# Second FFN of a one-layer decoder step: seven products in place of eight for two of three token chunks, parts kept in HBM between an up and a down phase

## Chip, cores and metric

One core of a Trainium2 chip. The metric is the device time of one execution in microseconds; of several executions the median counts.

## What is computed

One inference step of one layer, for a prompt of 1024 tokens and 8 single sample tokens, which share the weights: 1032 token rows of 1024 features.

```python
def swiglu(x, w_gate, w_up, w_down):
    return (jax.nn.silu(x @ w_gate) * (x @ w_up)) @ w_down

x = x + 0.5 * swiglu(rms_norm(x, g_ffn1), w1_gate, w1_up, w1_down)
proj = rms_norm(x, g_mix) @ w_in          # S5 branch, dilated attention, two gates
mixed = gate_ssm * (y_ssm @ w_ssm_proj) + gate_attn * (y_attn @ w_attn_proj)
x = x + mixed @ w_o
x = x + 0.5 * swiglu(rms_norm(x, g_ffn2), w2_gate, w2_up, w2_down)
```

The hidden width of both FFNs is 2816. Besides x the step returns key and value caches and S5 states. The change concerns the last line alone.

## The kernel before

Activations are feature-major: a tile xT holds 128 features on the partitions, 8 such blocks (KT), and 344 tokens (CH) in the columns; three chunks of 344 tokens make 1032. A float32 product is made as three matmuls of rounded parts (float32r): every operand is split into a high part (a cast on ScalarE) and a low part (the rest, a subtraction on VectorE), and high x high, high x low and low x high are added in PSUM (`mm3`, L148). Weights come in blocks of 512 KB through `loadw` (L131): a DMA from SP, the cast (L141), the subtraction (L142).

The step runs in stages: first FFN, mix (SSM, attention, gates, output projection `wo`), second FFN. The order of the instructions on each engine is set by a scheduler within the program's dependencies and the numbers of buffers.

In the mix stage's end `wo` (L1138 and following) adds the projection to chunk c of xT, and `wo_norm` (L1145) norms that chunk for the second FFN: squares on ScalarE, their sum over features by additions and one matmul with ones (`pT<-ss`, L120), a reciprocal root (`rsq`, L92), eight scalings (L127), and the split of each (L128, L129). It is called for chunk c right after `wo` of chunk c, so that it can stand beside the projection of the next chunk, or beside the FFN's first products.

`ffn` (L169) goes over 22 blocks f of 128 hidden features. `gateup(f)` makes gate and up products for three chunks: 2 x 8 x 3 x 3 = 144 matmuls of 128x344; the hidden block is split and stays in SBUF. After each pair of blocks `down` adds the pair before to all of xT: 8 x 3 x 2 x 3 = 144 matmuls per pair. The last `down` takes four blocks and goes chunk by chunk, and `store_x` (L939) turns each finished half of a chunk back to token-major by TensorE transposes (L950), copies (L951) and stores; six xr buffers.

## Time and profile before

| | us |
|---|---|
| median of 3 runs | 2418.6 (2417.37 to 2424.5) |
| profiled execution, its span | 2416.6 |
| TensorE busy | 2357.5 |
| VectorE busy | 1185.9 |
| ScalarE busy | 689.0 |
| GpSimd busy | 265.1 |

Of the profiled execution only the span is given; the median of the runs is 2.0 us above it. The second FFN begins at about 1660 us and ends with the kernel. How to read the views: a group gives one line's instructions of one shape with the mean of one; TensorE's matmuls overlap, so that the distance of their starts, not their mean, is what one takes in a stream. The chain of waits follows back, from the last instruction, what released each step.

### The profile page before, as it was taken

What the parts mean: (1) busy time and instruction counts of PE and PEld (TensorE: products, weight loads), DVE (VectorE), ACT (ScalarE), POOL (GpSimd) and SP (SyncE); (2) the same over time, 40 slices, a digit from 0 to 9 for tenths busy, and PEclk for the clock granted to TensorE, in tenths of its full rate; (3) what the DMA queues carried; (4) which work ended last, traced back from release to release, by engine and by line L of the source; (5) the groups of instructions that cost most, each with busy time, mean ns of one, the idle gap of its engine ahead of it and who ended that gap; (6) DMA issues with size and microseconds to landing.
All of it is one profiled execution on the core that took longest, in us unless ns stands there. A gap on an engine that the chain in (4) does not pass through costs nothing.

```text
span 2416.6 us, 37129 instructions
## 1 busy us (share of the span) xinstructions
PE 2357.5 (98%) x14805; PEld 2265.3 (94%) x14805; DVE 1185.9 (49%) x2690; ACT 689.0 (29%) x1364; POOL 265.1 (11%) x811
## 2 busy tenths in 40 slices
PE   7999999999999899989999999899999999999999
PEld 6999999999999799978887887899999999999999
DVE  7655544355442825555575535786234434433333
ACT  6211111111112433555444422345211111111111
POOL 2056766000001300000000000000000000000000
PEclk8999999999999899999999999999999999999999
DMA  5333434333233377551231246653111111111112
GB/s 140 97 111 104 128 95 130 105 94 113 82 110 102 128 202 232 164 157 45 80 108 46 63 135 199 188 159 92 45 43 53 48 40 53 44 44 53 50 39 71
DMA packets 279044, 241.24 MB, mean 100 GB/s; under 512 B 28958, under 2 KB 261054, under 8 KB 276694
## 3 DMA queue, kind: packets, MB, share of 16 engines
q1 hardware_dynamic: 274518, 190.66, 26.5%
q10 hardware_dynamic: 2816, 44.00, 6.0%
q0 software_dynamic: 1536, 4.21, 0.5%
q8 instruction: 116, 1.90, 0.3%
q14 instruction: 58, 0.48, 0.1%
HBM read 202.32 MB, written 80.49 MB: 117 GB/s over the span
## 4 chain that ended last, share of the span: by engine, by line
PE 90%; DMA 5%; DVE 3%; ACT 1%; issue 1%; SPq 0%; POOL 0%; DVEq 0%; ACTq 0%; POOLq 0%
PE pm L156 82%; PE ps L669 2%; DMA rs<-g_d 1%; PE acc L685 1%; PE pT L678 1%; PE pn L978 1%; DMA y_d<-Y 1%; DVE wl L142 1%; DMA num<-s_d 1%; DVE xn L127 0%; DMA raw<-in_w_in_dram 0%; DMA w<-w_d 0%; DMA xr<-in_x_prompt_dram 0%; PE pT L455 0%; PE pT L808 0%
## 5 line engine op out<-in xcount | busy, mean ns | idle before, releaser
L156 PE MATMUL pm<-al,wh 128*128 128x344 f32 x3280 | 1047.4, 323 | 2.1 <-DVE rs L1132 1.9
L156 PE MATMUL pm<-ah,wh 128*128 128x344 f32 x3152 | 1018.9, 323 | 9.3 <-ACT ah L128 3.8
L156 PE MATMUL pm<-ah,wl 128*128 128x344 f32 x2384 | 769.8, 323 | 2.3 <-DVE wl L142 2.3
L156 PEld LDWEIGHTS pm<-al,wh 128*128 128x128 f32 x3280 | 617.2, 189 | 12.8 <-issue 5.5
L156 PEld LDWEIGHTS pm<-ah,wh 128*128 128x128 f32 x3152 | 595.4, 189 | 19.1 <-issue 4.7
L156 PEld LDWEIGHTS pm<-ah,wl 128*128 128x128 f32 x2384 | 451.4, 189 | 9.7 <-issue 4.8
L141 ACT CAST wh<-raw 128x1024 fp32r<-128x1024 f32 (+1 forms) x220 | 220.4, 1009 | 730.6 <-PE pm L156 690.2
L142 DVE TENSOR_TENSOR wl<-raw,wh 128x1024 fp32r<-128x1024 f32 (+1 forms) x220 | 258.4, 1179 | 223.0 <-ACT wh L141 222.6
L198 DVE SCALAR_TENSOR_TENSOR xT<-pm,xT 128x344 f32<-128x344 f32 x480 | 243.9, 515 | 203.3 <-PE pm L156 203.1
L156 PE MATMUL pm<-hh,wh 128*128 128x344 f32 x1056 | 339.5, 322 | 0.0
L156 PE MATMUL pm<-hl,wh 128*128 128x344 f32 x1056 | 338.2, 320 | 0.0
L156 PE MATMUL pm<-hh,wl 128*128 128x344 f32 x1056 | 337.8, 321 | 0.0
L182 DVE TENSOR_TENSOR h<-h,pm 128x344 f32<-128x344 f32 x132 | 67.5, 512 | 450.6 <-PE pm L156 450.6
L156 PE MATMUL pm<-al,wl 128*128 128x344 f32 x832 | 265.1, 319 | 0.0
L156 PEld LDWEIGHTS pm<-hh,wh 128*128 128x128 f32 x1056 | 198.5, 188 | 0.3
L156 PEld LDWEIGHTS pm<-hl,wh 128*128 128x128 f32 x1056 | 198.4, 188 | 0.2
L156 PEld LDWEIGHTS pm<-hh,wl 128*128 128x128 f32 x1056 | 198.2, 188 | 0.1
L183 ACT CAST hh<-h 128x344 fp32r<-128x344 f32 x132 | 63.1, 478 | 333.4 <-DVE h L182 333.4
L156 PEld LDWEIGHTS pm<-al,wl 128*128 128x128 f32 x832 | 156.1, 188 | 0.1
L181 ACT ACTIVATE h<-pm 128x344 f32<-128x344 f32 x132 | 60.1, 456 | 220.8 <-PE pm L156 220.7
L184 DVE TENSOR_TENSOR hl<-h,hh 128x344 fp32r<-128x344 f32 x132 | 68.6, 520 | 40.0 <-ACT hh L183 39.9
L1133 POOL TENSOR_TENSOR rs<-rs,ah 128x344 f32<-128x344 f32 x3 | 2.8, 928 | 601.3 <-DVE rs L1132 601.3
(339 smaller groups left out, 2032.7 us busy)
## 6 DMA issues: line engine op xcount, KB each, us to landing
out_dram<-in_cache_kv_w_dram ACTq DMA_DIRECT2D x64, 512.0 KB
raw<-in_w_gate_dram SPq DMA_DIRECT2D x44, 512.0 KB
raw<-in_w_up_dram SPq DMA_DIRECT2D x44, 512.0 KB
raw<-in_w_down_dram SPq DMA_DIRECT2D x44, 512.0 KB
raw<-in_w_in_dram SPq DMA_DIRECT2D x38, 512.0 KB
raw<-in_w_o_dram SPq DMA_DIRECT2D x24, 512.0 KB
g_d<-gt SPq DMA_DIRECT2D x48, 172.0 KB
rs<-g_d SPq DMA_DIRECT2D x48, 172.0 KB
```

The source lines that it names most:

```text
L141: nc.scalar.copy(h[:, :k], raw[:, :k])
L142: nc.vector.tensor_sub(l[:, :k], raw[:, :k], h[:, :k])
L156: nc.tensor.matmul(p, w[:, kw], a[:, ka], start=first and i == 0, stop=last and i == n - 1)
L181: nc.scalar.activation(h, pg, AF.Silu)
L182: nc.vector.tensor_mul(h, h, pu)
L183: nc.scalar.copy(hh[:, c], h)
L184: nc.vector.tensor_sub(hl[:, c], h, hh[:, c])
L198: nc.vector.scalar_tensor_tensor(xT[c][:, m], p, 0.5, xT[c][:, m], op0=ALU.mult, op1=ALU.add)
L669: nc.tensor.matmul(p[h][:, :nk], qT[hs, s.block(g, b)], kT[hs, ks], start=True, stop=True)
L678: nc.tensor.transpose(pt[:, h, i], sm[:, h, 128 * i:128 * i + 128], s.ident)
L685: nc.tensor.matmul(acc[hs], vx[:, k, hs], P[:, h, i], start=i == 0, stop=i == nb - 1)
L978: nc.tensor.matmul(p2[:, :CH], s.bones, sq, start=True, stop=True)
```

## The change

The two chunks 0 and 1 are taken as the two column halves of a 2 x 2 block product, with the features (up) or the gate and up weights as the row halves, and the Strassen-Winograd form makes its 8 block products with 7, at the price of sums of operands and results. Chunk 2 is multiplied as before. Up: 7 x 4 x 3 = 84 matmuls for chunks 0 and 1 and 48 for chunk 2, 132 per block f instead of 144. Down: 132 instead of 144 per pair of blocks.

- `wo_norm` is called for all three chunks after `mix`, that is behind `wo` of chunk 2 in the program. It stores x to HBM (x_d), scales xT in place and makes nine split operands of 128x1376 columns (B11, B21, B22, T1 to T4 for chunks 0 and 1; D0, D1 for chunk 2). Three subtractions that GpSimd made are on VectorE.
- `wprep` makes for each f the sums S1 to S4 of the weights and splits them.
- `ffn_up` runs all 22 blocks. `second` makes, per pair of blocks, nine split parts of 128x688 and stores them to a new HBM tensor hs_d, 34.9 MB in all.
- `ffn_down` then runs three groups of 4, 4 and 3 pairs, each in nine runs (P1, P2, lo, hi, P4, P5, P6, P7, P3). A run reads its part back through a ring of four slots (`hload`), and adds into SBUF. In the last group the sums are combined, and `out` loads x again from x_d through one buffer y, adds, transposes and stores through two buffers xr.
- The pool of weight blocks `wp` is opened once for the first FFN and once for mix, instead of once for the kernel.

```diff
@@ run @@
             with ExitStack() as c4:
                 xT, tmp = s.mix(psum, c4)
-                psum(c4, 6, 2)
-                hpc = ExitStack()
-                hp = pool(hpc, "hp2", 4)
-                s.ffn(hp, tmp, i['w2_gate'], i['w2_up'], i['w2_down'], xT, lambda c, m: s.store_x(tmp, xT, c, m))
-                while copies:
-                    shift()
-                hpc.close()
+                s.ep = pool(ctx, "ep", side="right")
+                with ExitStack() as c5:
+                    s.wq = pool(c5, "wq", side="right")
+                    psum(c5, 6, 2)
+                    s.wprep(i['w2_gate'], i['w2_up'])
+                    for c in range(NCH):
+                        s.wo_norm(tmp, xT, c)
+                    c4.close()
+                    with ExitStack() as c6:
+                        s.ffn_up(pool(c6, "up2"))
+            with ExitStack() as c7:
+                psum(c7, 6, 2)
+                s.ffn_down(pool(c7, "wd", side="right"), pool(c7, "yo"), i['w2_down'])
+            while copies:
+                shift()
...
@@ mix @@
                 s.wo(tmp2, xT, 0)
                 s.attn_proj(tmp, oh, ol, 2)
-                s.wo_norm(tmp2, xT, 0)
                 for c in (1, 2):
                     s.wo(tmp2, xT, c)
-                    s.wo_norm(tmp2, xT, c)
         return xT, tmp2
...
+    SLOT = {'B11': 'al1', 'B21': 'ah2', 'B22': 'al2', 'T1': 'ah0', 'T2': 'e0', 'T3': 'e1', 'T4': 'e2', 'D0': 'ah1', 'D1': 'al0'}
+    def slot(s, name, sh, dt):
+        return (s.ep if name[0] == 'e' else s.act).tile(sh, dt, name=name)
+    def parts(s, x, hi, lo):
+        s.nc.scalar.copy(hi, x)
+        s.nc.vector.tensor_sub(lo, x, hi)
     def wo_norm(s, tmp, xT, c):
-        s.ah[c], s.al[c] = (s.act.tile([128, KT, CH], F32R, name=nm) for nm in (("al1", "ah2"), ("al2", "ah0"), ("ah1", "al0"))[c])
-        s.norm(tmp, c, 2, xT, s.ah, s.al)
+        nc = s.nc
+        V = nc.vector
+        nc.sync.dma_start(s.x_d[c], xT[c])
+        ss = tmp.tile([128, CH], F32, name="ss", bufs=1)
+        for k in range(KT):
+            if k == 0:
+                nc.scalar.activation(ss, xT[c][:, k], AF.Square)
+            else:
+                sq = tmp.tile([128, CH], F32, name="sq", bufs=2)
+                nc.scalar.activation(sq, xT[c][:, k], AF.Square)
+                V.tensor_add(ss, ss, sq)
+        p = s.pt.tile([128, 512], F32, name="pT")
+        nc.tensor.matmul(p[:, :CH], s.ones, ss, start=True, stop=True)
+        r = s.rsq(tmp, p[:, :CH], 1.0 / D)
+        for k in range(KT):
+            V.scalar_tensor_tensor(xT[c][:, k], xT[c][:, k], s.gains[:, 2, k:k + 1], r, op0=ALU.mult, op1=ALU.mult)
+        lo, hi = xT[c][:, 0:4], xT[c][:, 4:8]
+        def put(name, x):
+            s.ops[name] = t = s.slot(s.SLOT[name], [128, 2, 4, CH], F32R)
+            s.parts(x, t[:, 0], t[:, 1])
+        if c == 0:
+            s.ops, s.xn0 = {}, (lo, hi)
+            put('B11', lo)
+            put('B21', hi)
+        elif c == 1:
+            b11, b21 = s.xn0
+            V.tensor_sub(b11, lo, b11)
+            V.tensor_sub(lo, hi, lo)
+            put('B22', hi)
+            V.tensor_sub(hi, hi, b11)
+            put('T2', hi)
+            V.tensor_sub(b21, b21, hi)
+            put('T3', lo)
+            put('T1', b11)
+            put('T4', b21)
+        else:
+            put('D0', lo)
+            put('D1', hi)
...
+    def wprep(s, wg, wu):
...
+            put(('A11', 'A12'), g, "wg", 2)
+            V.tensor_add(S[0][:, 0:4], u[:, 0:4], u[:, 4:8])
+            V.tensor_sub(S[0][:, 4:8], S[0][:, 0:4], g[:, 0:4])
+            put(('S1', 'S2'), S[0], "wr", 1)
+            V.tensor_sub(S[1][:, 0:4], g[:, 0:4], u[:, 0:4])
+            V.tensor_sub(S[1][:, 4:8], g[:, 4:8], S[0][:, 4:8])
+            put(('S3', 'S4'), S[1], "wt", 1)
+            put(('A21', 'A22'), u, "wu", 1)
...
+    def ffn_up(s, ap):
...
+        def second(j, h1, h2):
+            def put(i, n, x):
+                t = ap.tile([128, 2, 2, CH], F32R, name="hs", bufs=2)
+                s.parts(x, t[:, :n, 0], t[:, :n, 1])
+                nc.sync.dma_start(s.hs_d[i:i + n, j].rearrange("i p z n -> p i (z n)"),
+                                  t[:, :n].rearrange("p i z n -> p i (z n)").bitcast(F32))
+            put(4, 2, h1[:, 0::2])
+            yield 1
+            T = ap.tile([128, 4, CH], F32, name="hT", bufs=1)
+            V.tensor_sub(T[:, 0], h1[:, 1], h1[:, 0])
+            V.tensor_sub(T[:, 1], h2[:, 1], T[:, 0])
+            yield 1
+            put(0, 2, T[:, 0:2])
+            yield 1
+            V.tensor_sub(T[:, 2], h2[:, 1], h1[:, 1])
+            V.tensor_sub(T[:, 3], h2[:, 0], T[:, 1])
+            yield 1
+            put(2, 2, T[:, 2:4])
+            yield 1
+            put(6, 2, h2[:, 0:2])
+            yield 1
+            put(8, 1, h2[:, 2:3])
...
+            a, b, c, d = bank(), None, None, None
+            s.mmk(a, W['A11'], O['B11'], 4)
+            p1 = u("p1")
+            nc.scalar.copy(p1, a)
+            b = bank()
+            s.mmk(b, W['S2'], O['T2'], 4)
+            U = u("U")
+            V.tensor_add(U, b, p1)
+            d = bank()
+            s.mmk(d, W['S3'], O['T3'], 4)
+            v = u("v")
+            V.tensor_add(v, d, U)
+            c = bank()
+            s.mmk(c, W['S1'], O['T1'], 4)
+            c22 = u("c22")
+            V.tensor_add(c22, c, v)
+            s.mmk(a, W['A12'], O['B21'], 4, False)
+            sl = u("sl", 2)
+            nc.scalar.activation(sl, a, AF.Silu)
+            s.mmk(d, W['A22'], O['T4'], 4, False)
+            c21 = u("cc", 2)
+            V.tensor_add(c21, d, U)
+            V.tensor_mul(h[:, 0], sl, c21)
+            s.mmk(c, W['S4'], O['B22'], 4, False)
+            c12 = u("cc", 2)
+            V.tensor_add(c12, c, U)
+            nc.scalar.activation(c12, c12, AF.Silu)
+            V.tensor_mul(h[:, 1], c12, c22)
...
+            if f % 2:
+                todo.append(second(f // 2, prev, h))
+            prev = h
+        step(20)
...
+    def ffn_down(s, wd, yo, w):
...
+        def hload(name, js):
+            nm = ('al2', 'e0', 'e1', 'e2')[hn[0] % 4]
+            hn[0] += 1
+            t = s.slot(nm, [128, 4, 2, CH], F32R)
+            nc.sync.dma_start(t[:, :len(js)].rearrange("p j z n -> p j (z n)").bitcast(F32),
+                              s.hs_d[HI[name], js[0]:js[0] + len(js)].rearrange("j p z n -> p j (z n)"))
+            return t
+        def run(terms, name, g):
+            p = [s.pm.tile([128, 512], F32, name="pm")[:, :CH] for _ in range(4)]
+            n = len(terms)
+            for e, (W, t, jj) in enumerate(terms):
+                for m in range(4):
+                    for z, (wz, az) in enumerate(((0, 0), (0, 1), (1, 0))):
+                        nc.tensor.matmul(p[m], W[wz][:, m], t[:, jj, az], start=e == 0 and z == 0, stop=e == n - 1 and z == 2,
+                                         skip_group_check=True)
+            acc = A[name]
+            for m in range(4):
+                if g == 0:
+                    (V.tensor_copy if m % 2 else nc.scalar.copy)(acc[:, m], p[m])
+                else:
+                    V.tensor_add(acc[:, m], p[m], acc[:, m])
+        def out(c, mh, x):
+            y = yo.tile([128, 4, CH], F32, name="y", bufs=1)
+            nc.sync.dma_start(y, s.x_d[c][:, 4 * mh:4 * mh + 4])
+            V.scalar_tensor_tensor(y, x, 0.5, y, op0=ALU.mult, op1=ALU.add)
+            for t0 in range(0, CH, 128):
+                n = min(128, CH - t0)
+                xr = yo.tile([128, 4, 128], F32, name="xr", bufs=2)
+                p = s.pt.tile([128, 4, 128], F32, name="pT")
+                for k in range(4):
+                    nc.tensor.transpose(p[:n, k], y[:, k, t0:t0 + n], s.ident)
...
+        for g, js in enumerate(GR):
+            last = g == len(GR) - 1
+            raw = []
+            for j in js:
+                r = []
+                for f in (2 * j, 2 * j + 1):
+                    x = wd.tile([128, D], F32, name="rd", bufs=9)
+                    nc.sync.dma_start(x, w[0][128 * f:128 * f + 128, :])
+                    s.shift()
+                    r.append(x)
+                raw.append(r)
+            half = (slice(0, 512), slice(512, 1024))
+            A1 = [wsplit(r[0][:, half[0]], "wa") for r in raw]
+            t = hload('P1', js)
+            run([(W, t, e) for e, W in enumerate(A1)], 'P1', g)
+            A2 = [wsplit(r[1][:, half[0]], "wb") for r in raw]
+            t = hload('P2', js)
+            run([(W, t, e) for e, W in enumerate(A2)], 'P2', g)
+            if last:
+                V.tensor_add(A['P2'], A['P1'], A['P2'])
+                out(0, 0, A['P2'])
...
+            for r, x in zip(raw, S):
+                V.tensor_sub(x, x, r[0][:, half[0]])
+            t = hload('P6', js)
+            run([(wsplit(x, "ws"), t, e) for e, x in enumerate(S)], 'P6', g)
...
+                V.tensor_add(A['P7'], A['P7'], A['P6'])
+                V.tensor_add(A['P4'], A['P4'], A['P7'])
+                out(0, 1, A['P4'])
+                V.tensor_add(A['P5'], A['P5'], A['P7'])
+                out(1, 1, A['P5'])
+            for r, x in zip(raw, S):
+                V.tensor_sub(x, r[1][:, half[0]], x)
+            t = hload('P3', js)
+            run([(wsplit(x, "ws"), t, e) for e, x in enumerate(S)], 'P3', g)
+            if last:
+                out(1, 0, A['P3'])
 def step_kernel(tc, *aps):
```

Three places show what the scheduler made of it. First TensorE at the passage from `wo` (L156 before, L157 after: matmuls of pm with ah, al) to the second FFN; pT<-ss is the sum of a norm. Before, around the last chunk's:

```order
L156 MATMUL pm<-al_16380,wl 128x344
L156 MATMUL pm<-al_16380,wh 128x344
L120 MATMUL pT<-ss,ones 128x344
L156 MATMUL pm<-ah_16381,wh 128x344
L156 MATMUL pm<-al_16380,wl 128x344
```

After, from the last two of `wo` of chunk 2 on (al_16985 is B11, e_17044 T2, e_17048 T3, ah_17051 T1):

```order
L157 MATMUL pm<-ah_16267,wh 128x344
L157 MATMUL pm<-al_16268,wh 128x344
L157 MATMUL pm<-ah_16267,wl 128x344
L1166 MATMUL pT<-ss,ones 128x344
L1241 MATMUL pm<-al_16985,wgh 128x344 x2
L1241 MATMUL pm<-al_16985,wgl 128x344
L1241 MATMUL pm<-al_16985,wgh 128x344 x2
L1241 MATMUL pm<-al_16985,wgl 128x344
L1241 MATMUL pm<-al_16985,wgh 128x344 x2
L1241 MATMUL pm<-al_16985,wgl 128x344
L1241 MATMUL pm<-al_16985,wgh 128x344 x2
L1241 MATMUL pm<-al_16985,wgl 128x344
```

Before, the last chunk's sum stands among the FFN's products of chunk 0, whose two parts al_16380 and ah_16381 are; after, the sums of chunks 1 and 2 stand behind all of `wo`, and of the FFN only the 12 products with B11 stand between them. On VectorE 61 instructions stand between the last addition of `wo` and the low part of D1; twelve of them, with the low parts of B22 (al_17040), T1 and T3 (xT_15754 and xT_15755 are chunks 0 and 1, S the weight sums, rs the root of chunk 2):

```order
L1182 TENSOR_TENSOR xT_15754<-xT_15755,xT_15754 128x1376
L1150 TENSOR_TENSOR al_17040<-xT_15755,al_17040 128x1376
L1225 TENSOR_TENSOR S_17121<-rw 128x512
L1221 TENSOR_TENSOR S_17120<-S_17120,rw 128x512
L102 TENSOR_TENSOR rs_17083<-rs_17083,rs_17085 128x344
L1183 TENSOR_TENSOR xT_15755<-xT_15755 128x1376
L1150 TENSOR_TENSOR ah_17051<-xT_15754,ah_17051 128x1376
L1226 TENSOR_TENSOR S_17121<-rw,S_17120 128x512
L103 TENSOR_SCALAR rs_17086<-rs_17083 128x344
L1185 TENSOR_TENSOR xT_15755<-xT_15755,xT_15754 128x1376
L1150 TENSOR_TENSOR e_17048<-xT_15755,e_17048 128x1376
L104 TENSOR_SCALAR rs_17085<-rs_17086 128x344
```

The wide sums of chunks 0 and 1 alternate with weight sums and with the steps of the last chunk's root; before, no instruction of 1376 columns stands here. Second, SP at the passage from up to down, after:

```order
L1267 DMA hs_d<-hs 128x2x688
L1380 DMA e_21565<-hs_d 128x4x688
L1380 DMA e_21623<-hs_d 128x4x688
L1380 DMA e_21625<-hs_d 128x4x688
L1380 DMA al_21491<-hs_d 128x4x688
L1267 DMA hs_d<-hs 128x2x688 x3
L1267 DMA hs_d<-hs 128x688
L1431 DMA rd<-in_w_down_dram 128x1024 x9
L1408 DMA y<-x_d 128x1376
L1380 DMA al_21867<-hs_d 128x4x688
L1380 DMA e_21933<-hs_d 128x4x688
L1431 DMA rd<-in_w_down_dram 128x1024 x2
```

The loads rd of the down weights stand behind the last pair's four stores to hs_d; before, the down weights of a pair stand among the loads of the next blocks. Third, TensorE's end, before:

```order
L156 MATMUL pm<-hh,wh 128x344
L156 MATMUL pm<-hl,wh 128x344
L156 MATMUL pm<-hh,wl 128x344
L950 MATMUL pT<-ident,xT_15751 128x128 x8
L950 MATMUL pT<-ident,xT_15751 88x128 x4
```

and after (e_23729 is the part of the last run, P3):

```order
L1396 MATMUL pm<-e_23729,wsh 128x344
L1396 MATMUL pm<-e_23729,wsl 128x344 x3
L1396 MATMUL pm<-e_23729,wsh 128x344
L1396 MATMUL pm<-e_23729,wsl 128x344
L1415 MATMUL pT<-ident,y 128x128 x8
L1415 MATMUL pT<-ident,y 88x128 x4
L1415 MATMUL pT<-ident,y 128x128 x8
L1415 MATMUL pT<-ident,y 88x128 x4
L1415 MATMUL pT<-ident,y 128x128 x8
L1415 MATMUL pT<-ident,y 88x128 x4
```

Before, 12 transposes stand behind the last product; after, 36, of three output halves, and the program loads y for the second and the third of them when the transposes of the one ahead have read it.

## Rows read from the trace of the kernel before

**Rows 1.** The page: span, busy time by engine, and the chain's shares by engine.

```profile
span 2416.6 us, 37129 instructions
...
PE 2357.5 (98%) x14805; PEld 2265.3 (94%) x14805; DVE 1185.9 (49%) x2690; ACT 689.0 (29%) x1364; POOL 265.1 (11%) x811
...
PE 90%; DMA 5%; DVE 3%; ACT 1%; issue 1%; SPq 0%; POOL 0%; DVEq 0%; ACTq 0%; POOLq 0%
```

**Rows 2.** Busy time by stretch: us; PE, PEld, DVE, ACT, POOL busy (count); clock, DMA share, GB/s.

```profile
1750.00:2400.00 650.00, 650.00 (x4153) 649.60 (x4153) 239.81 (x402) 106.87 (x169) 0.00 (x0) 1.00 0.16 48
```

**Rows 3.** The chain of waits in order of time: start, us, engine, line, count.

```profile
1662.31 705.58 PE pm L156 x4493
```

**Rows 4.** Timeline of TensorE: start us, us, instruction.

```profile
1599.69 0.32 PE L156 MATMUL pm<-al,wh 128*128 128x344 f32 x1
...
1630.40 0.32 PE L156 MATMUL pm<-al,wh 128*128 128x344 f32 x1
```

**Rows 5.** Groups by line, 1600 to 2417 us: busy us, mean ns of one, idle before.

```profile
L156 PE MATMUL pm<-al,wh 128*128 128x344 f32 x1176 | 374.8, 319 | 0.0
...
L198 DVE SCALAR_TENSOR_TENSOR xT<-pm,xT 128x344 f32<-128x344 f32 x240 | 122.1, 515 | 109.7 <-PE pm L156 109.7
...
L142 DVE TENSOR_TENSOR wl<-raw,wh 128x1024 fp32r<-128x1024 f32 x78 | 94.5, 1221 | 73.1 <-ACT wh L141 73.1
L141 ACT CAST wh<-raw 128x1024 fp32r<-128x1024 f32 x78 | 81.0, 1050 | 318.2 <-PE pm L156 312.4 <-DMA raw<-in_w_o_dram 5.8
...
L183 ACT CAST hh<-h 128x344 fp32r<-128x344 f32 x66 | 31.6, 478 | 163.4 <-DVE h L182 163.4
...
L127 DVE SCALAR_TENSOR_TENSOR xn<-xT,gains,rs 128x344 f32<-128x344 f32 x24 | 13.9, 598 | 0.1
L950 PE MATMUL pT<-ident,xT 128*128 128x128 f32 x48 | 8.7, 273 | 0.0
...
L118 DVE TENSOR_TENSOR ss<-ss,sq 128x344 f32<-128x344 f32 x14 | 7.8, 561 | 0.0
...
L104 DVE TENSOR_TENSOR rs<-rs,rs 128x344 f32<-128x344 f32 x3 | 1.5, 516 | 0.1
...
L102 DVE TENSOR_SCALAR rs<-rs 128x344 f32<-128x344 f32 x3 | 1.0, 335 | 0.1
```

**Rows 6.** The last chunk's second norm: its sum over features, then VectorE's last scaling.

```profile
L120 PE MATMUL pT<-ss,ones x12: 450/452/557, 781.5 to 1661.9; 128*128 128x344 f32 x12
...
1676.72 0.58 DVE L127 SCALAR_TENSOR_TENSOR xn<-xT,gains,rs 128x344 f32<-128x344 f32 x1
```

**Rows 7.** Timeline of TensorE after short waits in the mix stage.

```profile
1530.59 1.22 PE L156 MATMUL pm<-oh,wh 128*128 128x344 f32 x6 [1.93 <-ACT oh L1064]
...
1532.51 0.49 PE L156 MATMUL pm<-oh,wh 128*128 128x344 f32 x1
1532.80 0.49 PE L156 MATMUL pm<-ol,wh 128*128 128x344 f32 x1
...
1535.90 0.32 PE L156 MATMUL pm<-oh,wh 128*128 128x344 f32 x1
```

**Rows 8.** Transfers: two DMA waits of the chain (512 KB, 172 KB), one stretch's rate.

```profile
1041.42 5.99 DMA raw<-in_w_in_dram
...
1553.11 3.85 DMA rs<-g_d
...
1500.00:1514.00 14.00, 14.00 (x91) 14.00 (x90) 3.17 (x6) 0.84 (x2) 0.00 (x0) 1.00 0.98 382
```

**Rows 9.** Timeline of all engines after the last product.

```profile
2410.29 1.21 PE L950 MATMUL pT<-ident,xT 128*128 128x128 f32 x8
...
2410.49 0.52 DVE L198 SCALAR_TENSOR_TENSOR xT<-pm,xT 128x344 f32<-128x344 f32 x1 [1.81 <-PE pm L156]
...
2412.11 0.64 PE L950 MATMUL pT<-ident,xT 128*88 128x128 f32 x4 [0.61 <-ACT xr L951]
2412.83 0.58 ACT L951 COPY xr<-pT 88x512 f32<-88x512 f32 x1 [0.77 <-PE pT L950]
```

More of the change, by code (lines that the diff above doesn't have):

```diff
@@ L22 @@
 NF = DFF // 128
+NP = NF // 2
 EPS = 1e-6
@@ L838, in run @@
             s.x_d = tc.dram_tile([NCH, 128, KT, CH], F32, name="x_d")
+            s.hs_d = tc.dram_tile([9, NP, 128, 2, CH], F32, name="hs_d")
             s.cst = pool(ctx, "cst")
-            s.wp = pool(ctx, "wp")
             s.act = pool(ctx, "act")
@@ L870, in run @@
                 psum(c1, 6, 2)
+                s.wp = pool(c1, "wp", side="right")
                 xp, tmp = pool(c1, "xp"), pool(c1, "tmp", 2)
@@ L1006, in mix @@
         with ExitStack() as c2:
+            s.wp = pool(c2, "wp", side="right")
             aop = pool(c2, "aop", side="right")
@@ new lines, in wprep, with steps, put @@
+    def wprep(s, wg, wu):
+        V = s.nc.vector
+        s.W = [{} for _ in range(NF)]
+        def steps(f):
+            W = s.W[f]
+            raw = []
+            for w in (wg, wu):
+                r = s.wq.tile([128, KT, 128], F32, name="rw", bufs=3)
+                s.nc.sync.dma_start(r, w[0].rearrange("(k p) f -> p k f", p=128)[:, :, 128 * f:128 * f + 128])
+                s.shift()
+                raw.append(r)
+            g, u = raw
+            S = [s.wq.tile([128, KT, 128], F32, name=f"S{z}", bufs=1) for z in range(2)]
+            def put(names, x, nm, bufs):
+                h, l = (s.wq.tile([128, KT, 128], F32R, name=f"{nm}{z}", bufs=bufs) for z in "hl")
+                s.parts(x, h, l)
+                for k, n in enumerate(names):
+                    W[n] = h[:, 4 * k:4 * k + 4], l[:, 4 * k:4 * k + 4]
+            yield
+            put(('A11', 'A12'), g, "wg", 2)
+            yield
+            V.tensor_add(S[0][:, 0:4], u[:, 0:4], u[:, 4:8])
+            V.tensor_sub(S[0][:, 4:8], S[0][:, 0:4], g[:, 0:4])
+            yield
+            put(('S1', 'S2'), S[0], "wr", 1)
+            yield
+            V.tensor_sub(S[1][:, 0:4], g[:, 0:4], u[:, 0:4])
+            V.tensor_sub(S[1][:, 4:8], g[:, 4:8], S[0][:, 4:8])
+            yield
+            put(('S3', 'S4'), S[1], "wt", 1)
+            yield
+            put(('A21', 'A22'), u, "wu", 1)
+        s.prep = [steps(f) for f in range(NF)]
+        for _ in range(6):
+            next(s.prep[0], None)
```

131 lines of the change are left out of this document (114 added, 17 removed).

## Prediction

> **What bounds the kernel now.** I read the page first: TensorE is busy for 2357.5 of 2416.6 us and the chain that ended last is TensorE for 90%, line 156 alone for 82% [rows 1]. A share over the whole span says nothing of one stage, so next came the busy time by stretch: from 1750 us to 2400 us TensorE is busy in every microsecond, at full granted clock, while VectorE works for 240 of 650 us, ScalarE for 107, and the DMA engines have a share of 0.16 [rows 2]. The chain agrees: one piece of 705.58 us with 4493 matmuls, from 1662.31 on [rows 3]. So in the stage that is changed a removed matmul is removed time, and a wait that is put in TensorE's way is added time, whole. Nothing covers either. The stage holds no slack for TensorE now because every vector step is done under matmuls of something else: the norm of the last chunk, whose sum over features ran on TensorE at 1661.9, is still being scaled at 1676.72 while TensorE runs chunks 0 and 1 [rows 6].
>
> **Removed: 396 matmuls.** One pair of up-projection rounds falls from 288 to 264 matmuls (11 pairs: 264 fewer) and the down-projection from 144 to 132 per pair (132 fewer). The step from one 128x344 matmul to the next is the price, not the 319 ns of the groups, which overlap: 30.71 us for the 196 steps from 1599.69 to 1630.40 is 0.1567 us [rows 4]. 396 x 0.1567 = **-62.0 us**. The Trainium skill (TensorE: Matmul & The Clock Gate, Back-to-back issue gap) gives columns / 2.4 + 2.5 ns, here 146 ns as an estimate; the trace shows 157, and by the page's figure the gain would be 57.7 and my sum 4.3 us later.
>
> **Added 1: preparing the operands before the first product.** Norms and operand sums now come after the last output projection of all chunks. In the new order VectorE has 61 instructions between its last addition for chunk 2 and the low part of D1, and TensorE has only the first 12 products to do meanwhile. Durations from [rows 5]: a 128x344 sum takes 0.561 us, a 128x1024 one 1.221, so 0.97 ns a column; by that line 128x512 is 0.72 and 128x1376 is 1.56 (estimates). 16 scalings x 0.598 = 9.6; 11 wide sums and splits x 1.56 = 17.2; 6 weight splits x 1.221 = 7.3; 9 weight sums x 0.72 = 6.5; 7 additions of squares x 0.561 = 3.9; two reciprocal roots of 4 x 0.516 + 2 x 0.335, together 5.5. That is 50.0 us. It starts about 2 us late, behind ScalarE's two first steps of the root, so D1's low part is there at 52 and D0's at 49.7 us after the last projection. 82 matmuls of the first round stand behind D0's: 82 x 0.1567 = 12.9, end at 62.6. Its 134 matmuls need 21.0. TensorE loses 41.6 us. It also comes back slow: after 2 us of waits near 1531 the steps took 0.29 us in place of 0.157 from 1532.51 to 1535.90, where the matmuls' own time is back from 0.49 to 0.32: some 12 matmuls, 1.5 us [rows 7]. The Trainium skill (same page, Part 1: The HAM clock gate) calls the half rate the default that only activity lifts; the trace agrees, with that step at half rate; by it each new hole costs such a restart. Together **+43 us**. Bounds: if only the columns cost time (37,900 of them, 36.8 us) the loss is 29; if VectorE waits 6 us more for ScalarE it is 49.
>
> **Added 2: steady rounds of the up-projection.** A round has 132 matmuls, 20.7 us. VectorE has eight 344-column steps from PSUM at 0.515, four weight splits at 1.221, four weight sums at 0.72 and half of a pair's spill (3.2): 15 us, 73%. It hides; I take **+1**, 0 to 5.
>
> **Added 3: from up to down.** The loads of the first four pairs' down weights stand on SP behind the last spills, and these behind the last product. One product 0.51, one cast (0.77) and split (0.90) of 688 columns, one more split 0.56: the last spill is ready 2.9 us after the last up matmul, its issue and that of the first weight load bring 3.7. A load lands in 3.85 (172 KB) to 5.99 us (512 KB) [rows 8]; 4.7 taken for 512 KB in long rows, 8.4. The first two runs need eight weight splits, but the last of them is the 20th VectorE instruction: 20 x 0.72 = 14.5, at 22.9; 26 matmuls are left, 4.1, end 27.0. The 96 matmuls alone need 15.0. Lost: 12.0, with a slow restart **+13.5** (9 to 17).
>
> **Added 4: steady runs of the down-projection.** Per group of four pairs TensorE needs 528 x 0.1567 = 82.7 us; VectorE 48 half-width steps x 0.72 and 36 evacuations x 0.515 = 53. Reading back is 12.7 MB a group and the weights 4.2 MB, some 200 GB/s; 382 GB/s ran in the trace [rows 8]. Between runs the bank of the run before must be emptied while VectorE's queue holds splits: up to a microsecond where the order puts splits ahead. I take **+3** for 27 runs, 0 to 8.
>
> **Added 5: the tail.** Before, 12 transposes, a copy and a store follow the last product: 2410.29 to 2416.6, 6.3 us [rows 1, 9]. Now three output halves follow, through one buffer y that is loaded again from HBM each time. VectorE after the last matmul: 0.5 left over, four evacuations 2.1, two wide sums and a scale-add 4.7: 7.3. Each of the next two halves waits for TensorE to release y (1.7 after the scale-add, as 2411.0 to 2412.75 before), an issue of 0.4, a landing and a scale-add of 1.56. For a landing of 704 KB I take 5.2 (172 KB took 3.85; the other 532 KB at 382 GB/s 1.4); 3.85 and 6.5 bound it. 2 x 8.9 = 17.7. Then 2.4 to the last copy's end and 3.2 to the end as before. 30.6 - 6.3 = 24.3; but 24 transposes at 0.18 (8.7 us for 48) [rows 5] leave the busy stream, 4.3. **+20** (15 to 24).
>
> **Nothing:** the input x of the stage is stored from SBUF (three stores on SP, nobody waits), and the weight pool is opened twice. The first FFN's matmul order is unchanged; in the mix stage the order is shuffled, which I count as 0 within 8 either way: TensorE idles under 60 us in all there, and no row says which way a shuffle goes.
>
> **The sum.** -62.0 + 43 + 1 + 13.5 + 3 + 20 = +18.5 on the span of 2416.6, so 2435. The median of the runs is 2.0 above that span: **2437 us**.
>
> **Rivals.** (a) *Slower on top: the down phase waits for its own loads.* Weight loads of the next group are issued only when VectorE has made the last sum from the old rows, and splits of those new rows stand in VectorE's queue ahead of splits that the current group needs. Seven VectorE instructions, 4.6 us, lie between; the landing is 3.85 to 5.99 and the cast 0.6. If landings under load take 8 us more than this cover, two group changes cost 2 x 9: 2455. Against: each group has 29 us of VectorE slack. It decides from a landing of about 7 us. (b) *The preparation costs its lower bound*: 29 instead of 43, all else as forecast: 2423, no change that a measurement of this kernel can tell (0.3%, 7 us). For it: the start of a 128x1376 instruction is paid once, not three times, and my line through two sizes is only a line. (c) *Every hole at its lower end* (29 + 0 + 9 + 0 + 15 = 53): the removed matmuls win by 9 us, 2410 and, with a lucky shuffle in the mix stage, 2405. This is the faster side; for it speaks that three terms of mine are chains added up without overlap. (d) *The count alone*: no hole at all, 2357. Against it stand the orders: nothing else is left for TensorE at the three places.
>
> **How the numbers follow.** Forecast 0.50; (a) 0.17; (b) 0.18; (c) 0.13; (d) 0.02. Slower by over 0.3% is the forecast and (a), 0.67; within 0.3% (b), 0.18; faster (c) and (d), 0.15. The range takes in (c)'s and (a)'s values and little more: 2408 to 2458.
>
> **What would show it.** In the changed profile TensorE's matmul time should be 62 us less. Right after the last output projection there should be two holes with VectorE busy throughout, 40 us in sum, with the clock at its lower level behind the last. A thin stretch of about 27 us should stand where the first spilled part is read, and about 30 us after the last product with transposes in three bursts, a y load between them. If the down phase shows holes at its two group changes, it is (a). If VectorE finishes D1 in under 40 us, (b). If the first FFN or the mix stage differs by more than 8 us, my zero there is wrong.

## The result and the profile after

Four executions of the changed kernel gave a median of 2432.78 us (2430.95 to 2434.0) against 2420.34 for the kernel before beside it: ratio 1.0056 with a 95% interval of [1.0039, 1.0073]. It is slower by 12 us (0.5%), and the time lies 4 us under the forecast of 2437. The profiled execution has a span of 2431.7 us, 15.1 more than before. The page after (busy time and count by engine, the chain's shares, TensorE's busy share and clock in 40 slices):

```profile
span 2431.7 us, 37109 instructions
...
PE 2308.2 (95%) x14409; PEld 2209.9 (91%) x14409; DVE 1383.5 (57%) x2930; ACT 785.0 (32%) x1486; POOL 263.4 (11%) x808
...
PE   7999999999999899989999999895999999979996
...
PEclk8999999999999899999999999997999999989998
...
PE 88%; DVE 6%; DMA 4%; ACT 1%; issue 1%; SPq 0%; ACTq 0%; DVEq 0%
```

Beside [rows 1], TensorE has 396 matmuls fewer and is busy 49 us less, VectorE 198 us more, and TensorE's share of the chain is down by two points. The loss shows as three dents in TensorE's slices, near 1670, 2160 and 2410 us, and the clock dips at the same places. Outside of them nothing new is idle: from 1712 to 2145 us and from 2185 to 2399 TensorE is busy in every microsecond. The busy time by stretch of the second FFN (columns as in [rows 2]):

```profile
1658.60:1672.50 13.90, 4.66 (x14) 3.54 (x14) 13.90 (x24) 6.81 (x9) 0.00 (x0) 0.68 0.50 139
1672.50:1692.00 19.50, 6.79 (x27) 6.17 (x26) 19.46 (x21) 6.97 (x7) 0.00 (x0) 0.53 0.10 28
1692.00:1698.80 6.80, 2.62 (x16) 2.04 (x14) 6.76 (x12) 4.89 (x5) 0.00 (x0) 0.92 0.00 0
...
1698.78:1704.50 5.72, 5.72 (x20) 5.72 (x21) 4.11 (x6) 0.33 (x1) 0.00 (x0) 0.50 0.00 0
1704.50:1712.00 7.50, 7.50 (x49) 7.50 (x48) 1.44 (x3) 1.02 (x2) 0.00 (x0) 1.00 0.00 0
...
1712.00:2145.00 433.00, 433.00 (x2745) 433.00 (x2744) 287.94 (x421) 153.23 (x217) 0.00 (x0) 1.00 0.38 128
...
2152.00:2165.20 13.20, 0.12 (x2) 0.01 (x1) 2.58 (x5) 1.86 (x3) 0.00 (x0) 0.62 0.84 290
...
2185.00:2398.90 213.90, 213.90 (x1374) 213.63 (x1372) 121.03 (x204) 54.13 (x95) 0.00 (x0) 1.00 0.52 181
2398.90:2431.70 32.80, 8.77 (x38) 6.57 (x36) 11.29 (x12) 3.51 (x6) 0.00 (x0) 0.63 0.33 107
```

Ahead of the counts in brackets stand the busy times of TensorE, its weight loads, VectorE, ScalarE and GpSimd; the last three figures are clock, DMA share and GB/s. In the first three stretches VectorE is busy without a pause while TensorE has 14 of 40 us: the preparation of the operands. Behind them TensorE works throughout, at its lower clock level (0.50, which is 1.2 GHz) until about 1704.5 and at the upper one (1.00, 2.4 GHz) from there. From 2152 to 2165 us hardly anyone works but the DMA engines. In the last stretch all engines wait in turn.

The chain of waits names the works that end last there (start, us, what):

```profile
1667.62 3.49 DVE xT L1169 x7
...
1692.10 3.99 DVE xT L1169 x8
1697.15 1.59 DVE ah L1150
1698.78 445.77 PE pm L1241 x2806
2149.42 8.44 DMA hs_d<-hs
2159.37 5.13 DMA rd<-in_w_down_dram
2165.19 186.27 PE pm L1396 x1174
```

The low part of D0 (ah, L1150, at 1697.15) releases the long stream of the up-projection at 1698.78. At 2144.55 the chain leaves that stream for the last spills, while TensorE itself has up products until 2152; a store of spilled parts and a load of down weights follow.

For the comparisons below I divide the stage at TensorE's matmuls: the last of `wo`, the end of the first round f, the last of up, the 97th of down (behind the first two runs), the last of down.

| stretch (us) | changed kernel | what the products alone take | lost |
|---|---|---|---|
| last of `wo` to the end of the first round | 59.85 | 134 x 0.157 = 21.0 | 38.9 |
| 21 rounds of up | 437.56 | 2772 x 0.15675 = 434.5 | 3.0 |
| last of up to the 97th of down | 30.03 | 96 x 0.157 = 15.1 | 14.9 |
| rest of down, with 36 transposes | 216.93 | 216.9 | 0 |
| tail | 32.76 | 6.3 before, 2.7 for 24 transposes | 23.8 |

0.15675 us is the mean step of the gate and up products before, and 0.157 that of the whole stage before. The sum of the losses is 80.6; less 62.2 for 396 matmuls at 0.157 that makes 18.4. By its two ends the stage is 17.3 longer (759.9 before, 777.15 after; the third column is good to about a microsecond in sum), and `wo` ended 2.2 earlier in this execution: 15.1.

### The profile page after: what moved, and what is told of

Same layout as the page of the kernel before. It is cut to its first block, busy times and chain, and to the rows that moved or that the text cites. A ratio compares the mean times of both kernels' runs of the same rounds, so it can differ in the third digit from the quotient of the medians.

```text
span 2431.7 us, 37109 instructions
## 1 busy us (share of the span) xinstructions
PE 2308.2 (95%) x14409; PEld 2209.9 (91%) x14409; DVE 1383.5 (57%) x2930; ACT 785.0 (32%) x1486; POOL 263.4 (11%) x808
## 4 chain that ended last, share of the span: by engine, by line
PE 88%; DVE 6%; DMA 4%; ACT 1%; issue 1%; SPq 0%; ACTq 0%; DVEq 0%
PE pm L157 52%; PE pm L1241 18%; PE pm L1396 9%; PE ps L670 2%; PE acc L686 1%; DVE xn L128 1%; PE pT L679 1%; PE pn L969 1%; DMA raw<-in_w_in_dram 1%; DVE wl L143 1%; DMA xr<-in_x_prompt_dram 0%; DMA raw<-in_w_glu_dram 0%; PE pT L809 0%; PE pT L456 0%; DVE al L130 0%
## 5 line engine op out<-in xcount | busy, mean ns | idle before, releaser
L157 PE MATMUL pm<-al,wh 128*128 128x344 f32 x2224 | 709.8, 324 | 2.1 <-DVE rs L1122 1.4
L157 PE MATMUL pm<-ah,wh 128*128 128x344 f32 x2096 | 680.2, 325 | 3.9 <-ACT ah L129 1.9
L157 PE MATMUL pm<-ah,wl 128*128 128x344 f32 x2032 | 656.5, 323 | 0.0
L157 PEld LDWEIGHTS pm<-al,wh 128*128 128x128 f32 x2224 | 418.2, 189 | 10.7 <-issue 4.5
L157 PEld LDWEIGHTS pm<-ah,wh 128*128 128x128 f32 x2096 | 396.3, 189 | 14.6 <-issue 5.6
L157 PEld LDWEIGHTS pm<-ah,wl 128*128 128x128 f32 x2032 | 384.1, 189 | 7.1 <-issue 4.3
L199 DVE SCALAR_TENSOR_TENSOR xT<-pm,xT 128x344 f32<-128x344 f32 x240 | 121.8, 514 | 92.7 <-PE pm L157 92.5
L157 PE MATMUL pm<-hh,wh 128*128 128x344 f32 x528 | 169.8, 322 | 0.0
L157 PE MATMUL pm<-hl,wh 128*128 128x344 f32 x528 | 168.8, 320 | 0.0
L157 PE MATMUL pm<-hh,wl 128*128 128x344 f32 x528 | 168.3, 320 | 0.0
L157 PEld LDWEIGHTS pm<-hl,wh 128*128 128x128 f32 x528 | 99.3, 188 | 0.2
L157 PEld LDWEIGHTS pm<-hh,wh 128*128 128x128 f32 x528 | 99.2, 188 | 0.2
L157 PEld LDWEIGHTS pm<-hh,wl 128*128 128x128 f32 x528 | 99.1, 188 | 0.1
L1241 PEld LDWEIGHTS pm<-ah,wgh 128*128 128x128 f32 x352 | 62.2, 190 | 4.8 <-ACT ah L1149 2.5
```

The costliest lines, as they stand in the source:

```text
L157: nc.tensor.matmul(p, w[:, kw], a[:, ka], start=first and i == 0, stop=last and i == n - 1)
L199: nc.vector.scalar_tensor_tensor(xT[c][:, m], p, 0.5, xT[c][:, m], op0=ALU.mult, op1=ALU.add)
L1241: nc.tensor.matmul(p, W[w][:, k], B[:, a, k], start=first and k == 0 and z == 0, stop=k == n - 1 and z == 2, skip_group_check=True)
```

## Experiments

All kernels but one are variants of the changed one; that of experiment 5 is a variant of the kernel before. Ratios are to the kernel before on the same chip. Stretches are those of the table, each from one profiled execution. In the profiles in which a stretch was not edited the first one took 58.7 to 60.1 us, the passage from up to down 29.4 to 31.8 and the tail 32.5 to 33.1, so that a difference of 1 to 2 us in one of these says little.

**1. The norms of chunks 0 and 1 moved back under `wo`** (e1_early). Of the wide splits only those of T2, T3, T4 and the last chunk's stay behind the last projection.

```diff
-                    for c in range(NCH):
-                        s.wo_norm(tmp, xT, c)
+                    for name, x in s.late:
+                        s.put(name, x)
+                    s.wo_norm(tmp, xT, 2)
...
-                for c in (1, 2):
-                    s.wo(tmp2, xT, c)
+                s.late = []
+                s.wo_norm(tmp2, xT, 0)
+                s.wo(tmp2, xT, 1)
+                s.wo_norm(tmp2, xT, 1)
+                s.wo(tmp2, xT, 2)
...
```

> The changed kernel, with the norms and operand sums of chunks 0 and 1 (all but the splits of T2, T3, T4) put back behind their own output projection instead of behind all three. Theory (the hole at the passage is VectorE's work queued behind the last projection): of 44 us of VectorE work between the last projection and D0's low part some 28 remain, so the first round ends about 16 us earlier and the time falls from 2433 to about 2417 (2412 to 2421). Rival (the vector work is the load, its place is not): beside the last projection VectorE has 30 us in which 14 are taken and 18 would be added, so the projection slows down instead, and less than 5 us are won (2428 or more).

Measured: 2422.9 us, ratio 1.0017 [1.0007, 1.0026]. That is 2 us above the expected 2412 to 2421. The first stretch fell from 59.85 to 45.65, 14.2 us where 16 were looked for; `wo` itself ended about 2 us later, no more than its end differs by between executions, and the other stretches stayed within 1.3. Its chain of waits at the same place:

```profile
1681.38 3.05 DVE xT L1177 x7
1686.02 1.51 DVE ah L1154
1687.57 445.03 PE pm L1246 x2806
```

The stream starts 31 us after the last projection (1656.8) and not 44. So VectorE's work in that place makes the first hole, and moving work away shortens it nearly one for one; the rival, a slower projection and under 5 us won, did not come.

**2. The tail without its buffers' waits** (e2_y, e2_yx). First the last two output halves load their y into an operand slot that is dead by then; in the second kernel the xr of the last three halves also go through five places of another such slot. The first edit:

```diff
-            y = yo.tile([128, 4, CH], F32, name="y", bufs=1)
+            if c == 1:
+                if 'y2' not in A:
+                    t = s.slot('al1', [128, 2, 4, CH], F32)
+                    A['y2'] = [t[:, 0], t[:, 1]]
+                y = A['y2'].pop()
+            else:
+                y = yo.tile([128, 4, CH], F32, name="y", bufs=1)
```

> The changed kernel, with two more places for y (a dead accumulator tile), so that x of the last two output halves is loaded before the last product. Theory (the tail is the two loads of y behind the transposes, 4.5 us each): 9 to 10 us less, 2423. Rival (the two buffers xr, each held until its store has landed, take over as the pace of the tail): 3 to 6 us less, 2427 to 2430.

> The same, and xr of the last three output halves in five places of another dead tile. Theory (buffers alone make the tail): after the last product only two wide sums, three scale-adds, transposes, copies and one store remain, some 18 of 32.8 us, so 14 to 16 us less than the changed kernel, 2418. Rival (the copies and stores at the end are bound by DMA issue and landing whatever the buffers): no better than with two more y alone.

Measured: 2427.77 us, ratio 1.0038 [1.0024, 1.0052], tail 24.04 and so 8.7 shorter; with xr too 2424.05 us, 1.0024 [1.0013, 1.0035], tail 20.90, 11.9 shorter. The end of the chain of waits of the first of the two:

```profile
2407.21 1.61 DVE y L1415
...
2413.41 2.32 DMA out_dram<-xr
2416.62 2.04 DMA out_dram<-xr
2419.38 2.01 DMA out_dram<-xr
```

No load of y stands there any more. What is late next are the stores from the two xr buffers, which the second edit takes away; in all 11.9 us where 14 to 16 were looked for. By its time the first kernel falls into its rival's range (2427 to 2430), in part because the passage, which is not edited, was 1.8 us longer in its profile; the second missed its 2418 by 6 us. The profiled execution of the second had `wo` end at 1661.35, 6.8 us later than in the changed kernel's: the time ahead of the stage differs by several us from one execution to another, so the tail itself, not the span, is compared.

**3. The passage from up to down: one more spill buffer** (e3_hs3), **big loads later** (e8_late_d), **no spill** (e6_nospill).

```diff
-                t = ap.tile([128, 2, 2, CH], F32R, name="hs", bufs=2)
+                t = ap.tile([128, 2, 2, CH], F32R, name="hs", bufs=3)
```

> The changed kernel, with three buffers hs for the spill in place of two. Theory (the passage from up to down waits because the last spill waits for a buffer whose store stands beside four loads of 1376 KB): the last spill is ready some 3.5 us earlier and so are the weight loads behind it on SP: 3 to 4 us less, 2429 to 2430. Rival (the DMA engines are full, the weight loads land when the big loads are through): within 1 us of the changed kernel.

Measured: 2432.7 us, ratio 1.0061 [1.0048, 1.0073]; the passage to the 97th product 28.99 in place of 30.03. The third buffer is worth 1 us against that profile and 0.4 to 2.8 against the others: little, as the rival had it. Two pieces of its chain of waits, and then its busy time by stretch, show why:

```profile
2150.88 8.55 DMA hs_d<-hs
2160.95 4.17 DMA rd<-in_w_down_dram
```

```profile
2140.00:2150.00 10.00, 10.00 (x65) 10.00 (x64) 3.97 (x9) 1.72 (x3) 0.00 (x0) 1.00 1.01 368
2150.00:2160.00 10.00, 4.47 (x29) 4.18 (x27) 3.00 (x4) 2.27 (x4) 0.00 (x0) 0.86 1.01 376
```

The DMA share, the figure before the last, is 1: the DMA engines are full, and one buffer more is only filled sooner. The next kernel issues two of the four 1376 KB loads behind the first eight weight loads, where the order had put all four ahead of the last spills:

```diff
+            if g == 0:
+                first = hload('P1', js), hload('P2', js)
             for j in js:
...
-            t1, t2 = hload('d1', js), hload('d2', js)
+            t1, t2 = hload('d1', js, g == 0), hload('d2', js, g == 0)
```

> The changed kernel, with two of the four big loads at the passage from up to down (the parts of chunk 2, 1376 KB each, which the third run needs) moved on SP behind the first eight weight loads. Theory (the DMA engines are full at the passage: 5.6 MB of parts at 375 GB/s are 15 us, and the last spills and the weights land behind them): 2.8 MB less ahead, 5 to 7 us less, 2426. Rival (the spill buffers and the order of VectorE's splits set the passage): within 2 us of the changed kernel.

Measured: 2430.61 us, ratio 1.0049 [1.0036, 1.0062], which by itself is not clear of the changed kernel's 1.0056; the passage 26.05, 4.0 shorter than in the first profile (3.3 to 5.7 against the others), where 5 to 7 or under 2 were named. The store takes 4.64 us instead of 8.44, and the weights are issued 3.6 us after the last up product instead of 7.4:

```profile
2150.57 4.64 DMA hs_d<-hs
2156.74 4.65 DMA rd<-in_w_down_dram
```

Last, the parts are made and stored for the first four pairs only, and every read takes those; the parts of the other seven pairs are left out:

```diff
-            if f % 2:
+            if f % 2 and f < 8:
...
-                              s.hs_d[HI[name], js[0]:js[0] + len(js)].rearrange("j p z n -> p j (z n)"))
+                              s.hs_d[HI[name], 0:len(js)].rearrange("j p z n -> p j (z n)"))
```

> The changed kernel, but parts are made and stored for the first 4 of 11 pairs alone, and the down phase reads these for every group; the other 7 pairs' parts are left out. Theory (the passage from up to down waits for spills: stores, a buffer, and weight loads behind them on SP): with no spill near the passage the first product of the down phase stands 4 to 6 us after the last up matmul in place of 13, 8 to 10 us are won, 2423. The step of the up phase, 0.1578 us against 0.1568 in the kernel before, would fall to 0.157 from the ninth round on if the spill's traffic causes it, 1 to 2 us more. Rival (the weight loads wait for the four big loads alone, which are still there): 3 us or less.

Measured: 2425.71 us, ratio 1.0025 [1.0014, 1.0037]. The passage falls to 19.60, by 10.4 (9.8 to 12.2 against the others): of its 14.9 lost us 10.4 belong to the last pair's spill and the queue it stands in, 4.5 to the weights and splits behind it. The weights, issued from 2147.67 on behind the four big loads, still take 8.94 us, but most of that time now lies under the last up products.

```profile
1701.08 445.97 PE pm L1241 x2806
2147.67 8.94 DMA rd<-in_w_down_dram
```

The first row says a second thing: the long stream of up takes 445.97 us with seven of eleven spills left out and 445.77 with all. Its slower step, 0.1578 us, does not come from the spill.

**4. Twelve more matmuls in each round** (e4_extra), into a bank whose result nobody reads.

```diff
+            if f < NF:
+                px = bank()
+                s.mmk(px, W['S4'], O['B22'], 4)
```

> The changed kernel, with twelve more matmuls of 128x344 in each of the 22 up rounds, whose sum is not used: as many as the up phase had lost against the kernel before. Theory (TensorE sets the pace of the up phase and a matmul is worth its step): 264 x 0.157 = 41 us more, 2474 (2472 to 2476). Rival (VectorE's 15 us of 20.7 a round, in fixed order, set part of the pace): the added matmuls hide in part, 30 us or less; second rival (PSUM banks): the seventh bank of the round makes TensorE wait, 50 us or more.

Measured: 2469.77 us, ratio 1.0211 [1.0193, 1.023]. A round goes from 20.83 to 22.73 us, 0.1575 per added matmul, and the 21 rounds from 437.56 to 477.26. A matmul in the stream costs its step in full, and so a removed one should give it back: 62 us did come free. The time lies 2 us under the expected 2472 to 2476, because the first stretch got 3.7 us shorter although it holds twelve products more. The busy time by stretch around D0's low part shows how, first in the changed kernel (its stretch behind that is in the result above), then here:

```profile
1693.90:1698.78 4.88, 0.70 (x3) 0.30 (x2) 4.88 (x8) 4.86 (x5) 0.00 (x0) 0.89 0.00 0
```

```profile
1697.00:1699.00 2.00, 0.51 (x3) 0.23 (x3) 2.00 (x3) 2.00 (x3) 0.00 (x0) 1.00 0.00 0
...
1699.00:1712.00 13.00, 13.00 (x82) 13.00 (x83) 7.82 (x11) 4.57 (x8) 0.00 (x0) 1.00 0.00 0
```

In the changed kernel TensorE has 0.7 us of work in the 4.9 us ahead of the 82 products that need D0's low part, and these begin at a clock of 0.50 and take 15.6 us. Here twelve products more run ahead of them, the wait just before is down to 1.5 us, the clock stays at 1.00, and the 82 take 13.0. The other 1.1 us are a weight split that stands behind D0's low part in this order and not ahead of it.

**5. The kernel before, with its three norms behind all of `wo`** (e7_before_late): the moved place alone, without operand sums.

```diff
+                for c in range(NCH):
+                    s.wo_norm(tmp, xT, c)
...
-                s.wo_norm(tmp2, xT, 0)
                 for c in (1, 2):
                     s.wo(tmp2, xT, c)
-                    s.wo_norm(tmp2, xT, c)
```

> The kernel before, with its three norms for the second FFN behind all three output projections, as the change has them, and nothing else. Theory (the hole at the passage is the wide operand sums of two chunks and the splits behind them, not the norms' place alone): products of chunk 0 cover most of chunk 1's norm (12 us of VectorE against 7.5 us of matmuls), so 4 to 9 us are lost, 2423 to 2427. Rival (the place alone): 25 us or more, 2444.

Measured: 2426.14 us, ratio 1.003 [1.0017, 1.0043], 6.6 us longer, within the 4 to 9 expected; the first 144 products take 31.6 us from the last projection on, in place of 23.2, 8.4 more. In this row TensorE is busy for 25.8 of 30 us and VectorE for 24.6:

```profile
1660.00:1690.00 30.00, 25.79 (x141) 23.16 (x140) 24.56 (x47) 16.07 (x30) 1.94 (x2) 0.94 0.00 1
```

So the place of the norms alone costs 7 to 8 us where the products of chunk 0 can run meanwhile. The other 30 us of the first hole come with the sums and splits that the seven products need, and behind which all but the first 12 products stand. The two parts need not add up, since the order differs: putting norms and sums back together won 14.2 us in experiment 1.

**6. All mends together** (e5_all: 1, both of 2, the third buffer and the late loads) **beside the changed kernel once more** (after_again).

> The changed kernel with all four edits: norms and sums of chunks 0 and 1 behind their own projections, spare places for y and xr in the tail, three buffers hs, the two parts of chunk 2 behind the first weight loads. Theory (three holes in three places, each with its own cause, so that what was won in the stretches adds): 14.2 at the first passage, 11.9 in the tail, 4 to 6 at the second, less 2 that the earlier norms cost ahead: 28 to 30 us less than the changed kernel, 2403 to 2406, and 13 to 16 below the kernel before. Rival (the edits share a cause, DMA or VectorE, so that they do not add): 2412 or more.

> The changed kernel itself, on the chip of this comparison: 2431 to 2434, 12 to 15 above the kernel before; its stretches (last projection to the end of the first round, the up rounds, the passage, the down runs, the tail) within 0.5 us of the first profile's, the time ahead of the last projection within 4 us.

Measured: 2407.16 us, ratio 0.9947 [0.9933, 0.996], against 2436.41, 1.007 [1.0056, 1.0083], on the same chip. Both lie above what was expected (2403 to 2406 and 2431 to 2434), their difference of 29 us within the 28 to 30. The changed kernel's executions here lay 3.6 us higher than at first, and in its profile `wo` ended 3.8 us later (1658.3).

```profile
span 2406.1 us, 37108 instructions
...
PE 2308.1 (96%) x14409; PEld 2209.4 (92%) x14409; DVE 1380.7 (57%) x2930; ACT 784.1 (33%) x1486; POOL 262.5 (11%) x808
```

The first stretch is 46.17 (59.81 in the profile of the second measurement), the passage 25.43 (30.61), the tail 20.19 (32.50): 31 us less in three places, 0.8 more in the rest of down. With the same arithmetic this version beats the kernel before by 11 us. The losses that are left are 25 + 3 + 10 + 1 + 11 = 50 against 62 gained.

## Why the prediction was right, and where its terms were off

**Removed, -62.0: measured -62.2.** That is the count at the mean step of the stage before, and the added matmuls of experiment 4 give nearly the same price. The step of [rows 4] was the right one to take. The sign that I had named for it, 62 us less matmul time, did not come: TensorE's busy time fell by 49, since it is busy for 30.4 us in the first stretch, where its products need 21.0 at the upper clock level, and 3.0 us longer in the rounds of up.

**Preparation, +43: measured 38.9.** The mechanism is the one forecast, and experiment 1 shows it. D0's low part was there 44.2 us after the last projection, not 49.7. The failed step is the price of a VectorE instruction: I refused the overlapping duration for TensorE and took it for VectorE. VectorE's timeline of after (start, us, instruction):

```profile
1677.34 0.68 DVE L1225 TENSOR_TENSOR S<-rw 128x512 f32<-128x512 f32 x1
1677.94 0.68 DVE L1221 TENSOR_TENSOR S<-S,rw 128x512 f32<-128x512 f32 x1
1678.55 0.50 DVE L102 TENSOR_TENSOR rs<-rs,rs 128x344 f32<-128x344 f32 x1
1678.97 1.58 DVE L1183 TENSOR_TENSOR xT<-xT 128x1376 f32<-128x1376 f32 x1
1680.47 1.58 DVE L1150 TENSOR_TENSOR ah<-xT,ah 128x1376 fp32r<-128x1376 f32 x1
```

Each starts 0.08 us before its forerunner's recorded end: 0.60 for 512 columns where I had 0.72, 1.50 for 1376 where I had 1.56, and 0.49 for a scaling where I had 0.598. Over some 60 instructions that is the 5 us. The Trainium skill (VectorE: DVE Perf Modes, The DRAIN you can't avoid) says that the next operation does not start until the pipe is empty, and that one that is not held starts earlier; in these rows the starts stand ahead of the recorded ends. The other way went the slow restart: the 82 products behind D0 took 15.6 us and not 12.9, with the first 5.7 us at a granted clock of 0.50 (1.2 GHz) and the rest at 1.00 (2.4 GHz). I had 1.5 us for it, from a place where TensorE had waited for 2 us; here it had worked little for 40. In experiment 4, where the clock stayed up, the 82 took 13.0. The two holes of 40 us that I had named as the sign came as six waits, 29.4 us in sum, the longest 12.7 and 8.4; the rest of the 38.9 is products at the lower level.

**Steady up, +1: measured +3.0.** No round waits: each takes 20.83 us. It is a step of 0.1578 us instead of 0.1567, over 2772 matmuls. I looked for waits and found a price. With most of the spill left out it is the same (experiment 3). Nor is it new: in the kernel before the gate and up products step 0.1567 us, but the down products 0.1577, and the down products after 0.1571. What makes it is open.

**Up to down, +13.5: measured 14.9, by another mechanism.** I had the last spill's work follow freely (in 2.9 us, though the four steps that I named add up to 2.7), the first down product some 9.0 us after the last up product, and then 18.0 for 96 matmuls that VectorE's splits hold back, with 1.5 for a slow restart. The first product came at 13.2 and the 96 in 16.8, of which 15.1 are their steps. SP's timeline there:

```profile
2135.10 7.94 SPq L1380 DMA_DIRECT2D e<-hs_d  x3
...
2144.57 0.36 SPq L1380 DMA_DIRECT2D al<-hs_d  x1
...
2159.37 5.69 SPq L1431 DMA_DIRECT2D rd<-in_w_down_dram  x9
```

And the compute engines':

```profile
2152.22 0.51 DVE L1348 TENSOR_TENSOR h<-sl,pm 128x344 f32<-128x344 f32 x1 [2.83 <-PE pm L1241]
2156.18 0.77 ACT L1149 CAST hs<-h 128x688 fp32r<-128x688 f32 x1 [7.34 <-DMA hs_d<-hs]
...
2165.19 2.66 PE L1396 MATMUL pm<-al,wah 128*128 128x344 f32 x8 [13.08 <-ACT wah L1149]
```

The last hidden block is ready at 2152.7, but its cast waits until 2156.18 for a spill buffer whose store is not through, and the last part's for the next store, that of 8.44 us. Ahead of these stores the four loads of spilled parts, 5.6 MB, had been issued from 2135 on, and the DMA engines were full (busy time by stretch):

```profile
2144.00:2150.00 6.00, 6.00 (x40) 6.00 (x39) 4.14 (x7) 2.39 (x4) 0.00 (x0) 1.00 1.01 362
2150.00:2156.00 6.00, 2.12 (x14) 1.83 (x12) 0.51 (x1) 0.00 (x0) 0.00 (x0) 0.92 1.00 382
```

The order that I printed ahead of the forecast has these loads ahead of the last stores; I read it for the weights alone and missed that an early load of data for later is a late store of what is needed now. Experiment 3 settles it: with fewer loads ahead the store is shorter and the first product earlier, and without the last spill the wait is gone. The Trainium skill (DMA: Bandwidth & Descriptors, Queues, rings and completion order) says that SP owns one ring on each DMA engine, and that each engine consumes descriptors in ring order; the store's 8.44 us against 4.64 with two loads fewer ahead agree. The thin stretch behind it, where VectorE's splits were to hold TensorE back, did not come: the two errors partly cancel, so the near total says nothing for the step.

**Steady down, +3: measured 0.** TensorE has no gap from 2185 to 2399, not even at the group changes. Rival (a), weights that come late there, did not occur.

**Tail, +20: measured 23.8.** Timeline after the last product:

```profile
2403.35 1.58 DVE L1409 SCALAR_TENSOR_TENSOR y<-ah,y 128x1376 f32<-128x1376 f32 x1
2405.08 2.85 PE L1415 MATMUL pT<-ident,y 128*128 128x128 f32 x12 [6.00 <-DVE y L1409]
2408.22 0.38 SPq L1408 DMA_DIRECT2D y<-x_d  x1
...
2412.84 1.59 DVE L1409 SCALAR_TENSOR_TENSOR y<-ah,y 128x1376 f32<-128x1376 f32 x1 [5.10 <-DMA y<-x_d]
...
2427.86 0.58 ACT L1416 COPY xr<-pT 88x512 f32<-88x512 f32 x1 [2.14 <-DMA out_dram<-xr]
```

Each of the two repeated halves takes 9.49 us (8.9 forecast): the load came back a microsecond sooner than I had it, and the transposes (2.85 us for 12) released y a microsecond and a half later. VectorE's start took 6.0, not 7.3. Two terms were missed or mis-sized: the last copy waits 2.14 us for one of the two xr buffers, which I had left out, and the 24 transposes gave back 2.7 of the busy stream and not 4.3, since one takes 0.11 us from the next there and not the 0.18 that busy time by count made. Experiment 2 shows the y wait (8.7 us) and the xr wait (3.1 more).

**Nothing elsewhere, 0 within 8: -2.2.** That is the end of `wo`, and within what it differs by between executions. That the total came so near is in part luck: terms that were 4 too high (preparation) and 3 (steady down) stand against terms that were 2 (steady up), 1.4 (passage) and 3.8 (tail) too low. The sign did not hang on that: the holes cost 81 us and would have had to fall below 62. Rivals (b) to (d) needed a preparation near 29 us or no holes; it cost 39.

## To carry to other kernels

When fewer matmuls are bought with sums and with parts that pass through memory, price the count at the step of the stream, then go to each place where the new stage begins, changes phase and ends: there the vector work stands alone, and three such places outweighed a 62 us gain. Put the preparation under the matmuls of the stage ahead, keep TensorE supplied right up to the long stream so that it does not begin it at the lower clock (13.0 us in place of 15.6 in experiment 4), keep loads for later out of the queue in front of the stores that the last products wait for, and give the last outputs buffers that are dead by then: here this turned 12 to 18 us of loss into 11 us of gain with the same arithmetic. And take the distance of starts as the price of an instruction on VectorE too, not its duration.

## What the runs showed of the hardware

- Float32r matmuls of 128x344 had a steady step of 0.1567 us in one loop and 0.1578 in another of the same shape, at a granted clock of 1.00 with no gap in either; leaving out spills changes nothing of it, and twelve matmuls added to each round cost 0.1575 each. Two other loops of the same shape had 0.1577 and 0.1571. The cause stays open.
- A 688 KB store behind 5.6 MB of loads from the same queue took 8.44 us (up to 9.22 in other profiles) at a DMA share of 1.0 and 362 to 382 GB/s; with half the loads ahead 4.64.
- While TensorE had 6.8 of 19.5 us of work, its granted clock was 0.53 on average. After 8 us of steady work and then 0.7 us of work in 4.9 it began the next stream at 0.50 and reached 1.00 after 5.7 us; after 9.8 us of work in 9.9 and then 0.5 in 2.0 it began it at 1.00 (experiment 4).
- The time ahead of the changed stage differs by up to 7 us between executions of programs that are nearly the same there (last projection at 1654.6 to 1661.4), more than some of the effects studied here.
